# Layer 0's per-layer embedding computed in the even mixer ahead of its state scan, stored in DRAM and read back in the tail

## The chip, the cores and the metric

The program runs on one core of one Trainium2 chip. The metric is the device time of one execution in microseconds. The kernel before took 1391.22 us in the median of three runs (1390.14 to 1392.95). The engines are named as the profile names them: PE is the TensorE matmul engine (PEld its weight load), DVE the VectorE, ACT the ScalarE, POOL the GpSimd, SP the SyncE, whose queue issues nearly all DMAs here.

## The reference, cut to what matters

One inference step of a two-layer encoder over two groups of tokens that share the weights: 512 prompt rows and 32 sample rows, together T = 544 columns of width D = 1024, in float32. Layer 0 has the even mixer, layer 1 the odd one; each layer then has a causal ConvFFN and the gated per-layer embedding.

```python
for i in range(DEPTH):
    hn = rmsnorm(h, W['g_mix_pre'][i])
    # layer 0, the even mixer
    z = hn @ W['w_even_in'][j]
    gb, gc, xa, u = jnp.split(z, [A_WIDTH, 2 * A_WIDTH, 3 * A_WIDTH], axis=-1)
    yc, new_hist = causal_dwconv(gc * xa, hist, W['w_conv_a'][j])
    ya = gb * yc
    yb, nr, ni = s5_mixer(u, h0r, h0i, ...)      # complex diagonal scan, then GLU
    y = jnp.concatenate([ya, yb], axis=-1) @ W['w_even_out'][j]
    ...
    h = h + rmsnorm(y, W['g_mix_post'][i])
    hn = rmsnorm(h, W['g_ffn_pre'][i])
    up = hn @ W['w_ffn_up'][i]
    uc, new_f = causal_dwconv(up, fh, W['w_ffn_conv'][i])
    gt, val = jnp.split(uc, 2, axis=-1)
    y = (jax.nn.gelu(gt) * val) @ W['w_ffn_down'][i]
    h = h + rmsnorm(y, W['g_ffn_post'][i])
    h = h + jax.nn.sigmoid(h @ W['w_ple_gate'][i]) * (pe[i] @ W['w_ple'][i])
```

The change concerns the last factor, `pe[i] @ W['w_ple'][i]` (256 by 1024 weights), for layer 0. It depends on inputs alone.

## The kernel before

Activations lie with features on the partitions and the 544 columns in two halves of 256 and 288 (HALVES). Every float32 product is made from split operands: x = Xh + Xl and w = wh + wl in a rounded format, and each step of the contraction is three matmuls of 128 by 128 weights (L131 Xh with wh, L132 Xl with wh, L133 Xh with wl). A job (mm_job) is one output tile of 128 features for one half: with K = 8 steps 24 matmuls into one PSUM tile `ps`. A list of units (L53) gives the order in which weights are fetched: `prefetch` (L92) brings one unit over SP's queue into `raw`, ACT rounds it to `wh` (L107), DVE makes `wl` (L108).

`phase` (L166) runs the jobs of one matrix product: both halves, the second some jobs (delta) behind the first, and a consumer that evicts a job's PSUM tile a few jobs later (lag). Other work is written as generators in a task list; `run(n)`, called after each job, takes n steps of the list, so that the scan's small pieces are spread between jobs. The framework then reorders each engine's instructions somewhat before it fixes them: an engine issues in one fixed order, and waits on semaphores.

The even mixer (layer 0) has these parts in the program. The u jobs: phase of 4 tiles with c_u, 8 jobs in both halves. Then a shuffle of 16 DMAs brings u into the layout of the scan (L917). Then the scan is put on the task list (L897 to L915): prep_g makes G (L821) and PE transposes it (`tb`, L826); front multiplies u by the input matrix (`v`, L858) and scans on DVE (`rt` L867, `rg`, L875, `sp` L878); prep_c makes the output matrix Cm for five powers tau (products and sums `Tm` on DVE, L789 and L791, copied by ACT, L794); prep_t multiplies Cm by g on PE (`tp`, L837) and fills the matrix Tm (L840, L845); back applies Cm and Tm on PE (`yp`, L891 and L893). The a jobs: phase of 12 tiles with c_a, 24 jobs, which carry the scan's pieces between them. When both are through, the GLU (`GG`, L978) follows, and the output projection.

In the tail of each layer the ConvFFN's down jobs end with a residual for each half: a norm (`rp` on PE, L307 with ones and L314 with a transpose), and eight steps k on DVE and ACT, each of y (L338), h (L339), Xh (L323) and Xl (L325). Xh and Xl of a half feed the gate jobs, 24 matmuls each, one step of the contraction for each k. Between down and gate stands the embedding (L455 to L474): 16 jobs of two steps, 6 matmuls each, evicted by ACT with a factor 0.5 into `e` (L472).

Of the kernel before, what the change touches and what calls it, by code (L numbers as in the profile page):

```python
# [8 lines left out]
F32 = mybir.dt.float32  # L9
F32R = mybir.dt.float32r  # L10
# [41 lines left out]

def units():  # L53

    u = [("w_even_in", i, 8) for i in range(16)]
    u += [("w_glu", i, 8) for i in range(2)]
    u += [("w_even_out", i, 8) for i in range(8)]
    for layer in range(2):
        for p, (a, b) in enumerate(FF_PARTS):
            u += [("w_up%d" % layer, i, 8) for i in range(2 * a, 2 * b)]  # L60
            u += [("w_down%d_%d" % (layer, p), i, b - a) for i in range(8)]
        u += [("p", layer, 8)]
        u += [("w_ple%d" % layer, i, 8) for i in range(2)]
        u += [("w_gate%d" % layer, i, 8) for i in range(8)]
        if layer == 0:
            u += [("w_odd_in", i, 8) for i in range(21)]
            u += [("w_odd_out", i, 8) for i in range(8)]
    return u
# [3 lines left out]
def trunk_kernel(ctx: ExitStack, tc: tile.TileContext, A: dict):  # L72
# [4 lines left out]
    main = ctx.enter_context(tc.tile_pool(name="main", bufs=1))  # L77
    small = ctx.enter_context(tc.tile_pool(name="small", bufs=2))
    mm = ctx.enter_context(tc.tile_pool(name="mm", bufs=3, space=PSUM))


    ulist = units()
# [246 lines left out]
    def residual(half, h, y, st, gpost, gnext, rB=None):  # L329
# [18 lines left out]
            rB[half] = yield from s2.fin(D)  # L348
        waiting.discard(("r", half))


    def out_proj(layer, h, y, rB):

# [14 lines left out]
    def tail(layer, h, next_g):  # L368
# [2 lines left out]

        fs = ExitStack()
        ff = fs.enter_context(tc.tile_pool(name="ff%d" % layer, bufs=2))
        wscope(8 + 2 * NG + 24 + 11, fs.enter_context(tc.tile_pool(name="wf%d" % layer, bufs=4)))
        psc["extra"] = fs.enter_context(tc.tile_pool(name="fp%d" % layer, bufs=4, space=PSUM))
        psc["of"] = (7, 2)
        psc["st"] = fs.enter_context(tc.tile_pool(name="fs%d" % layer, bufs=1, space=PSUM))
# [11 lines left out]
        out_proj(layer, h, new_y(), rB)  # L389
        y = new_y()  # L390


        ps_r = ff.tile([128, 2, T - SEQ], F32, tag="psr", name="psr", bufs=1)
        nc.sync.dma_start(ps_r, A["ps"][layer])


        cg = [{}, {}]
# [6 lines left out]
        for p, (f0, f1) in enumerate(FF_PARTS):  # L404
            gt = [[ff.tile([128, 8, w], F32R, tag="g%d%s" % (half, s), name="g%s" % s, bufs=1)
                   for s in "hl"] for half, (_, w) in enumerate(HALVES)]

            def c_up(half, i, ps, f0=f0, gt=gt):
                w = HALVES[half][1]
                f, kind = f0 + i // 2, i % 2  # L410
                ct = f + NG * kind
                U = ff.tile([128, UW], F32, tag="U", name="U", bufs=3)
                vec.tensor_tensor(block_view(U, half)[2], like(ps, half), like(rB[half], half), op=OP.mult)  # L413
                history(U, half, hca[:, ct], hcs[:, layer, ct])
                if half == 0:
                    pool_e.tensor_copy(hca[:, ct], U[:, 256:258])  # L416
                t = ff.tile([128, T - 256], F32, tag="ct%d" % kind, name="t", bufs=2)
                t = t[:, :w]
                taps(U, half, t, lambda j: conv_w(j, ct))
                if half == 1:  # L420
                    ends(U, fout[:, layer, ct].rearrange("p (a b) -> p a b", a=2))
                if kind == 0:
                    act.activation(t, t, AF.Gelu_apprx_tanh)  # L423
                    cg[half][f] = t
                else:
                    g = cg[half].pop(f)
                    vec.tensor_tensor(g, g, t, op=OP.mult)  # L427
                    gh, gl = gt[half]
                    act.activation(gh[:, f - f0], g, AF.Copy)  # L429
                    vec.tensor_tensor(gl[:, f - f0], g, gh[:, f - f0], op=OP.subtract)  # L430

            phase(2 * (f1 - f0), 8, src_x, c_up, delta=6, rate=2, lag=6 if p == 0 else 1)

            def c_down(half, j, ps, p=p):
                yk = y[half][:, j]
                if p == 0:
                    act.activation(yk, ps, AF.Copy)
                else:
                    vec.tensor_tensor(yk, yk, ps, op=OP.add)  # L439
                if p == len(FF_PARTS) - 1:  # L440
                    st[half].add(yk)

            def a_down(half):
                def f():
                    task(residual(half, h, y[half], st[half], ("g_ffn_post", layer), None),
                         ("x", half), ("r", half))
                return f

            last = p == len(FF_PARTS) - 1
            phase(8, f1 - f0, lambda half, gt=gt: (gt[half][0], gt[half][1], 0), c_down, delta=6, rate=2, lag=4,  # L450
                  after=(a_down(0), a_down(1)) if last else (None, None))
        nc.sync.dma_start(A["o_ffn"][:, layer], fout[:, layer])


        us = take(3)  # L455
        prefetch(us[2])
        pA = [w_[:, :].rearrange("p (k t) c -> p k (t c)", k=2) for w_ in loaded[us[0]]]
        pB = [[ff.tile([128, T - 256], F32R, tag="ct%d" % i, name="pB", bufs=2) for k in range(2)] for i in range(2)]
        for k in range(2):
            for i in range(2):  # L460
                act.activation(pB[i][k][:, 0:256], pA[i][:, k, 256:512], AF.Copy)
            act.activation(pB[0][k][:, 256:], ps_r[:, k], AF.Copy)
            vec.tensor_tensor(pB[1][k][:, 256:], ps_r[:, k], pB[0][k][:, 256:], op=OP.subtract)
        emb = []
        for half, (c0, w) in enumerate(HALVES):
            e = ff.tile([128, 8, w], F32, tag="g%dh" % half, name="e", bufs=1)
            emb.append(e)
            xs = pA if half == 0 else pB
            for j in range(8):
                ps = ps_tile()  # L470
                mm_job(ps, us[1 + j // 4], range(2), xs[0], xs[1], 0, w, k0=2 * (j % 4))
                act.activation(e[:, j], ps[:, :w], AF.Copy, scale=0.5)  # L472
                run(j % 2)
        prefetch(us[2] + wsc["ring"])  # L474

        st = [Stat(0), Stat(1)]

# [40 lines left out]
    def mixer_even(h):  # L518
# [376 lines left out]
                           AF.Gelu_apprx_tanh)  # L895

        def scan():  # L897
            yield from prep_g(0)
            yield from prep_g(1)
            for s in range(10):  # L900
                if s >= 2:
                    back(s - 2)
                    yield
                if s == 5:
                    shuffle(True, (0, 1))
                if s < 8:
                    front(s)
                    yield
                    if s == 0:
                        yield from prep_c()  # L910
                    if s % 2 == 0:
                        yield from prep_t(s // 2)
                    elif s < 5:
                        yield from prep_g(s // 2 + 2)
            shuffle(True, (2, 3))  # L915
# [10 lines left out]
        task(discretize())  # L926
        phase(4, 8, src_x, c_u, delta=4, rate=3, lag=4)
        shuffle(False, (0, 1, 2, 3))
        task(scan())


# [423 lines left out]
        ms.close()  # L1355


    wscope(18)
    h = new_h()
    for half, (c0, w) in enumerate(HALVES):  # L1360
        for k0 in range(0, 8, 2 if half == 0 else 4):
# [157 lines left out]
```

## Time and profile before

| | us |
|---|---|
| runs | 1392.95, 1391.22, 1390.14 (median 1391.22) |
| profiled execution, its own time | 1392.53 |
| its span, first to last instruction | 1390.8 |
| PE busy | 1367.2 (98%) |
| DVE busy | 935.7 (67%) |
| ACT busy | 657.4 (47%) |
| mean granted PE clock | 0.996 of full speed |

The profile is one execution. A row of its timeline gives the start of an instruction (or of a run of equal ones), its length, the engine, the line of the kernel, the operation, the tiles written and read, the size and the count; in square brackets stands the idle time before it and what ended that. Matmuls overlap, so a job's length is read from the start of its first matmul to the start of the next job's first. Lines are those of the kernel before unless the kernel after is named.

### The profile page before, as it was taken

What the parts mean: (1) busy time and instruction counts of PE and PEld (TensorE: products, weight loads), DVE (VectorE), ACT (ScalarE), POOL (GpSimd) and SP (SyncE); (2) the same over time, 40 slices, a digit from 0 to 9 for tenths busy, and PEclk for the clock granted to TensorE, in tenths of its full rate; (3) what the DMA queues carried; (4) which work ended last, traced back from release to release, by engine and by line L of the source; (5) the groups of instructions that cost most, each with busy time, mean ns of one, the idle gap of its engine ahead of it and who ended that gap; (6) DMA issues with size and microseconds to landing.
All of it is one profiled execution on the core that took longest, in us unless ns stands there. A gap on an engine that the chain in (4) does not pass through costs nothing.

```text
span 1390.8 us, 27437 instructions
## 1 busy us (share of the span) xinstructions
PE 1367.2 (98%) x10859; PEld 1344.2 (97%) x10859; DVE 935.7 (67%) x1968; ACT 657.4 (47%) x1314; POOL 198.3 (14%) x621
## 2 busy tenths in 40 slices
PE   8899999999999999999999999999999999999998
PEld 8798999999999999999998998999999999999998
DVE  9998738983477546868655555479843676368682
ACT  6653545543344223445547755465433343234451
POOL 1000000431022201300131100012320123013000
PEclk9999999999999999999999999999999999999999
DMA  6322352232312231331332332331223123313321
GB/s 199 94 67 63 117 184 77 77 96 72 122 62 86 97 122 39 105 113 53 99 94 70 117 109 64 108 107 62 92 92 122 46 92 107 99 50 94 100 73 50
DMA packets 49376, 128.26 MB, mean 92 GB/s; under 512 B 8368, under 2 KB 19896, under 8 KB 48992
## 3 DMA queue, kind: packets, MB, share of 16 engines
q1 hardware_dynamic: 47456, 124.35, 28.0%
q0 software_dynamic: 1792, 2.17, 0.7%
q8 instruction: 85, 1.39, 0.4%
q14 instruction: 43, 0.35, 0.1%
HBM read 116.93 MB, written 4.76 MB: 88 GB/s over the span
## 4 chain that ended last, share of the span: by engine, by line
PE 87%; DVE 8%; ACT 2%; SPq 1%; DMA 1%; issue 1%; POOL 0%; ACTq 0%; DVEq 0%
PE ps L131 27%; PE ps L133 27%; PE ps L132 27%; DVE wl L108 1%; SPq L924 1%; PE av L1254 1%; PE rp L307 1%; DVE Xl L327 1%; PE pp L1243 1%; DVE rg L875 1%; DVE rt L877 1%; ACT wh L107 1%; PE sc L1230 1%; DVE y L338 0%; DMA h<-in_x 0%
## 5 line engine op out<-in xcount | busy, mean ns | idle before, releaser
L131 PE MATMUL ps<-Xh,wh 128*128 128x256 f32 (+1 forms) x2512 | 728.1, 290 | 1.8 <-ACT wh L107 1.1
L133 PE MATMUL ps<-Xh,wl 128*128 128x256 f32 (+1 forms) x2512 | 725.5, 289 | 2.0 <-DVE wl L108 2.0
L132 PE MATMUL ps<-Xl,wh 128*128 128x256 f32 (+1 forms) x2512 | 725.6, 289 | 0.8 <-DVE Xl L327 0.5
L131 PEld LDWEIGHTS ps<-Xh,wh 128*128 128x128 f32 x2512 | 473.9, 189 | 4.4 <-ACT wh L107 1.6
L132 PEld LDWEIGHTS ps<-Xl,wh 128*128 128x128 f32 x2512 | 474.7, 189 | 3.0 <-DVE Xl L327 1.2
L133 PEld LDWEIGHTS ps<-Xh,wl 128*128 128x128 f32 x2512 | 473.0, 188 | 2.5 <-DVE wl L108 2.4
L108 DVE TENSOR_TENSOR wl<-raw,wh 128x1024 fp32r<-128x1024 f32 (+2 forms) x214 | 256.9, 1201 | 151.3 <-ACT wh L107 149.5
L107 ACT ACTIVATE wh<-raw 128x1024 fp32r<-128x1024 f32 (+2 forms) x214 | 222.1, 1039 | 248.3 <-PE ps L132 232.9
L131 PE MATMUL ps<-gh,wh 128*128 128x288 f32 (+1 forms) x704 | 203.5, 289 | 0.0
L133 PE MATMUL ps<-gh,wl 128*128 128x288 f32 (+1 forms) x704 | 203.4, 289 | 0.0
L132 PE MATMUL ps<-gl,wh 128*128 128x288 f32 (+1 forms) x704 | 202.5, 288 | 0.0
L132 PEld LDWEIGHTS ps<-gl,wh 128*128 128x128 f32 x704 | 133.5, 190 | 0.0
L131 PEld LDWEIGHTS ps<-gh,wh 128*128 128x128 f32 x704 | 133.0, 189 | 0.0
L133 PEld LDWEIGHTS ps<-gh,wl 128*128 128x128 f32 x704 | 132.9, 189 | 0.0
L278 ACT ACTIVATE t<-U,prm 128x256 f32<-128x256 f32 (+1 forms) x176 | 90.4, 517 | 71.0 <-DVE U L413 67.5
L279 DVE SCALAR_TENSOR_TENSOR t<-U,prm,t 128x256 f32<-128x256 f32 (+1 forms) x176 | 87.2, 498 | 34.9 <-ACT t L278 34.7
L413 DVE TENSOR_TENSOR U<-ps,rB 128x256 f32<-128x256 f32 (+1 forms) x176 | 76.6, 437 | 23.9 <-PE ps L133 19.8
L280 DVE SCALAR_TENSOR_TENSOR t<-U,prm,t 128x256 f32<-128x256 f32 (+1 forms) x176 | 87.5, 501 | 4.5
L416 POOL COPY hca<-U 128x2 f32<-128x2 f32 x88 | 24.3, 277 | 366.2 <-DVE U L413 366.1
L423 ACT ACTIVATE t<-t 128x288 f32<-128x288 f32 (+1 forms) x88 | 37.7, 429 | 81.6 <-DVE t L280 81.5
L439 DVE TENSOR_TENSOR y<-y,ps 128x256 f32<-128x256 f32 (+1 forms) x64 | 27.9, 436 | 62.0 <-PE ps L133 62.0
L429 ACT ACTIVATE gh<-t 128x288 fp32r<-128x288 f32 (+1 forms) x88 | 37.4, 425 | 67.3 <-DVE t L427 67.3
(272 smaller groups left out, 1376.7 us busy)
## 6 DMA issues: line engine op xcount, KB each, us to landing
raw<-in_w_up SPq DMA_DIRECT2D x88, 512.0 KB, 3.4
raw<-in_w_down SPq DMA_DIRECT2D x32, 512.0 KB, 3.4
raw<-in_w_odd_in SPq DMA_DIRECT2D x21, 512.0 KB, 3.6
raw<-in_w_gate SPq DMA_DIRECT2D x16, 512.0 KB, 4.0
raw<-in_w_even_in SPq DMA_DIRECT2D x15, 512.0 KB, 3.7
raw<-in_w_down SPq DMA_DIRECT2D x16, 384.0 KB, 3.1
raw<-in_w_even_out SPq DMA_DIRECT2D x8, 512.0 KB, 4.0
raw<-in_w_odd_out SPq DMA_DIRECT2D x8, 512.0 KB, 3.5
```

Of the source, the lines that this page charges most:

```text
L107: act.activation(wh[:, k], raw[:, k], AF.Copy)
L108: vec.tensor_tensor(wl[:, k], raw[:, k], wh[:, k], op=OP.subtract)
L131: pe.matmul(ps[:, :n], wh[:, k0 + k, :], h_, start=(i == 0), stop=False)
L132: pe.matmul(ps[:, :n], wh[:, k0 + k, :], l_, start=False, stop=False)
L133: pe.matmul(ps[:, :n], wl[:, k0 + k, :], h_, start=False, stop=(i == last))
L278: act.activation(t, v[2], AF.Copy, scale=w(2))
L279: vec.scalar_tensor_tensor(t, v[1], w(1), t, op0=OP.mult, op1=OP.add)
L280: vec.scalar_tensor_tensor(t, v[0], w(0), t, op0=OP.mult, op1=OP.add)
L413: vec.tensor_tensor(block_view(U, half)[2], like(ps, half), like(rB[half], half), op=OP.mult)
L423: act.activation(t, t, AF.Gelu_apprx_tanh)
L429: act.activation(gh[:, f - f0], g, AF.Copy)
L439: vec.tensor_tensor(yk, yk, ps, op=OP.add)
```

## The change

The embedding of layer 0 moves out of the tail. Its units (the input `p` and two of `w_ple0`) come after the four units of the u jobs. A function `embed` now holds the products for both layers. For layer 0 it is called in the even mixer after the u jobs and the shuffle, ahead of `task(scan())` and of the a jobs; with halves of 288 and 256 columns; each of its 16 jobs is evicted by ACT into a small tile `e` (three buffers), stored by an SP DMA into a DRAM tensor `emb0`, and takes one step of the task list. In the tail of layer 0 two DMAs read `emb0` back into the tiles that the gate uses. Layer 1 keeps its embedding where it was.

`scan` begins with three empty steps of the task list, so its pieces come three steps later. In the last down phase of layer 0 the consumer runs two jobs behind instead of four.

```diff
@@ -52,15 +52,19 @@
 
 def units():
 
-    u = [("w_even_in", i, 8) for i in range(16)]
+    u = [("w_even_in", i, 8) for i in range(4)]
+    u += [("p", 0, 8)]
+    u += [("w_ple0", i, 8) for i in range(2)]
+    u += [("w_even_in", i, 8) for i in range(4, 16)]
     u += [("w_glu", i, 8) for i in range(2)]
     u += [("w_even_out", i, 8) for i in range(8)]
     for layer in range(2):
         for p, (a, b) in enumerate(FF_PARTS):
             u += [("w_up%d" % layer, i, 8) for i in range(2 * a, 2 * b)]
             u += [("w_down%d_%d" % (layer, p), i, b - a) for i in range(8)]
-        u += [("p", layer, 8)]
-        u += [("w_ple%d" % layer, i, 8) for i in range(2)]
+        if layer == 1:
+            u += [("p", 1, 8)]
+            u += [("w_ple1", i, 8) for i in range(2)]
         u += [("w_gate%d" % layer, i, 8) for i in range(8)]
         if layer == 0:
             u += [("w_odd_in", i, 8) for i in range(21)]
@@ -77,6 +81,8 @@
     main = ctx.enter_context(tc.tile_pool(name="main", bufs=1))
     small = ctx.enter_context(tc.tile_pool(name="small", bufs=2))
     mm = ctx.enter_context(tc.tile_pool(name="mm", bufs=3, space=PSUM))
+    dram = ctx.enter_context(tc.tile_pool(name="dram", bufs=1, space=bass.MemoryType.DRAM))
+    emb0 = dram.tile([128, 8, T], F32, tag="emb0", name="emb0")
 
 
     ulist = units()
@@ -348,6 +354,25 @@
             rB[half] = yield from s2.fin(D)
         waiting.discard(("r", half))
 
+    def embed(ps_, pB, n0, put):
+
+        us = take(3)
+        prefetch(us[2])
+        pA = [w_[:, :].rearrange("p (k t) c -> p k (t c)", k=2) for w_ in loaded[us[0]]]
+        m = SEQ - n0
+        for k in range(2):
+            for i in range(2):
+                act.activation(pB[i][k][:, 0:m], pA[i][:, k, n0:SEQ], AF.Copy)
+            act.activation(pB[0][k][:, m:T - n0], ps_[:, k], AF.Copy)
+            vec.tensor_tensor(pB[1][k][:, m:T - n0], ps_[:, k], pB[0][k][:, m:T - n0], op=OP.subtract)
+        for n, (c0, w) in enumerate(((0, n0), (n0, T - n0))):
+            xs = pB if n else pA
+            for j in range(8):
+                ps = ps_tile()
+                mm_job(ps, us[1 + j // 4], range(2), xs[0], xs[1], 0, w, k0=2 * (j % 4))
+                put(n, j, c0, w, ps[:, :w])
+        prefetch(us[2] + wsc["ring"])
+
 
     def out_proj(layer, h, y, rB):
 
@@ -371,7 +396,7 @@
 
         fs = ExitStack()
         ff = fs.enter_context(tc.tile_pool(name="ff%d" % layer, bufs=2))
-        wscope(8 + 2 * NG + 24 + 11, fs.enter_context(tc.tile_pool(name="wf%d" % layer, bufs=4)))
+        wscope(8 + 2 * NG + 24 + (11 if layer else 8), fs.enter_context(tc.tile_pool(name="wf%d" % layer, bufs=4)))
         psc["extra"] = fs.enter_context(tc.tile_pool(name="fp%d" % layer, bufs=4, space=PSUM))
         psc["of"] = (7, 2)
         psc["st"] = fs.enter_context(tc.tile_pool(name="fs%d" % layer, bufs=1, space=PSUM))
@@ -389,9 +414,10 @@
         out_proj(layer, h, new_y(), rB)
         y = new_y()
 
-
-        ps_r = ff.tile([128, 2, T - SEQ], F32, tag="psr", name="psr", bufs=1)
-        nc.sync.dma_start(ps_r, A["ps"][layer])
+        if layer:
+
+            ps_r = ff.tile([128, 2, T - SEQ], F32, tag="psr", name="psr", bufs=1)
+            nc.sync.dma_start(ps_r, A["ps"][layer])
 
 
         cg = [{}, {}]
@@ -447,31 +473,25 @@
                 return f
 
             last = p == len(FF_PARTS) - 1
-            phase(8, f1 - f0, lambda half, gt=gt: (gt[half][0], gt[half][1], 0), c_down, delta=6, rate=2, lag=4,
+            phase(8, f1 - f0, lambda half, gt=gt: (gt[half][0], gt[half][1], 0), c_down, delta=6, rate=2,
+                  lag=2 if last and layer == 0 else 4,
                   after=(a_down(0), a_down(1)) if last else (None, None))
         nc.sync.dma_start(A["o_ffn"][:, layer], fout[:, layer])
 
 
-        us = take(3)
-        prefetch(us[2])
-        pA = [w_[:, :].rearrange("p (k t) c -> p k (t c)", k=2) for w_ in loaded[us[0]]]
-        pB = [[ff.tile([128, T - 256], F32R, tag="ct%d" % i, name="pB", bufs=2) for k in range(2)] for i in range(2)]
-        for k in range(2):
-            for i in range(2):
-                act.activation(pB[i][k][:, 0:256], pA[i][:, k, 256:512], AF.Copy)
-            act.activation(pB[0][k][:, 256:], ps_r[:, k], AF.Copy)
-            vec.tensor_tensor(pB[1][k][:, 256:], ps_r[:, k], pB[0][k][:, 256:], op=OP.subtract)
-        emb = []
-        for half, (c0, w) in enumerate(HALVES):
-            e = ff.tile([128, 8, w], F32, tag="g%dh" % half, name="e", bufs=1)
-            emb.append(e)
-            xs = pA if half == 0 else pB
-            for j in range(8):
-                ps = ps_tile()
-                mm_job(ps, us[1 + j // 4], range(2), xs[0], xs[1], 0, w, k0=2 * (j % 4))
-                act.activation(e[:, j], ps[:, :w], AF.Copy, scale=0.5)
+        emb = [ff.tile([128, 8, w], F32, tag="g%dh" % half, name="e", bufs=1) for half, (_, w) in enumerate(HALVES)]
+        if layer == 0:
+            for half, (c0, w) in enumerate(HALVES):
+                nc.sync.dma_start(emb[half], emb0[:, :, c0:c0 + w])
+        else:
+            pB = [[ff.tile([128, T - 256], F32R, tag="ct%d" % i, name="pB", bufs=2) for k in range(2)]
+                  for i in range(2)]
+
+            def put_e(n, j, c0, w, ps):
+                act.activation(emb[n][:, j], ps, AF.Copy, scale=0.5)
                 run(j % 2)
-        prefetch(us[2] + wsc["ring"])
+
+            embed(ps_r, pB, 256, put_e)
 
         st = [Stat(0), Stat(1)]
 
@@ -895,6 +915,8 @@
                            AF.Gelu_apprx_tanh)
 
         def scan():
+            for _ in range(3):
+                yield True
             yield from prep_g(0)
             yield from prep_g(1)
             for s in range(10):
@@ -926,6 +948,19 @@
         task(discretize())
         phase(4, 8, src_x, c_u, delta=4, rate=3, lag=4)
         shuffle(False, (0, 1, 2, 3))
+
+
+        ps_r = s5.tile([128, 2, T - SEQ], F32, tag="psr", name="psr")
+        nc.sync.dma_start(ps_r, A["ps"][0])
+        pB = pt([128, 2, 2, 256], "pB").bitcast(F32R)
+
+        def put_e(n, j, c0, w, ps):
+            e = small.tile([128, T - 256], F32, tag="sq", name="e", bufs=3)[:, :w]
+            act.activation(e, ps, AF.Copy, scale=0.5)
+            nc.sync.dma_start(emb0[:, j, c0:c0 + w], e)
+            run(1)
+
+        embed(ps_r, [[pB[:, i, k] for k in range(2)] for i in range(2)], 288, put_e)
         task(scan())
 
 
@@ -1355,7 +1390,7 @@
         ms.close()
 
 
-    wscope(18)
+    wscope(21)
     h = new_h()
     for half, (c0, w) in enumerate(HALVES):
         for k0 in range(0, 8, 2 if half == 0 else 4):
```

Line numbers of the kernel after: matmuls L137 to L139, `rp` L313 and L320, `tb` L846, `tp` L857, `v` L878, `Cm` copies L814, evictions of the embedding `e` L959, `so` L900.

PE at the start of the even mixer, before: the u jobs end with the first row, then six a jobs with `tb` and `v` between them, then `tp`.

```order
L133 MATMUL ps<-Xh,wl 128x288
L131 MATMUL ps<-Xh,wh 128x256 [waits DVE_49,PE_49,Activation_49]
...
L826 MATMUL tb<-cst,G 128x128 [waits PE_49,Activation_49]
...
L858 MATMUL v<-UUh,Bm 128x137 x2
...
L837 MATMUL tp<-Cm,g_707 32x128 [waits Activation_49]
L837 MATMUL tp<-Cm,g_707 32x128 x7
```

The same place after: behind the u jobs stand the embedding's jobs (`ps<-wh` for the first 288 columns, `ps<-pB` for the other 256), then `tp`, and only then the first a job.

```order
L139 MATMUL ps<-Xh,wl 128x288
L137 MATMUL ps<-wh 128x288 [waits DVE_49,Activation_49]
...
L137 MATMUL ps<-pB,wh 128x256 [waits Activation_49]
...
L846 MATMUL tb<-cst,G 128x128 [waits Activation_49]
...
L139 MATMUL ps<-pB,wl 128x256
L857 MATMUL tp<-Cm,g_957 32x128 [waits Activation_49]
L857 MATMUL tp<-Cm,g_957 32x128 x5
L137 MATMUL ps<-Xh,wh 128x256 [waits Activation_49]
```

What moved: before, 6 of the 24 a jobs stand ahead of the first `tp` on PE; after, none does, and the embedding's 96 matmuls stand there instead.

ACT at the copies of Cm that `tp` waits for, before: two copies for each power tau, close together.

```order
L794 ACTIVATE Cm<-Tm 64x32x16 [waits DVE_49]
L794 ACTIVATE Cm<-Tm 64x32x16
L107 ACTIVATE wh<-raw 128x1024 [waits DMAHW5_49,PE_49]
L794 ACTIVATE Cm<-Tm 64x32x16 [waits DVE_49]
L794 ACTIVATE Cm<-Tm 64x32x16
L880 ACTIVATE so<-sp 128x2x2x2 [waits DVE_49]
```

After, evictions `e` of the embedding stand between them, each waiting for a DMA (the store that frees its buffer).

```order
L814 ACTIVATE Cm<-Tm 64x32x16 [waits DVE_49]
L959 ACTIVATE e<-ps 128x256 [waits DMAHW6_49,Activation_49]
L959 ACTIVATE e<-ps 128x256 [waits DMAHW7_49,Activation_49]
L959 ACTIVATE e<-ps 128x256 [waits DMAHW0_49,PE_49,Activation_49]
L900 ACTIVATE so<-sp 128x2x2x2 [waits DVE_49]
L814 ACTIVATE Cm<-Tm 64x32x16
```

What moved: three evictions of the embedding and one copy of the scan's state stand between the two Cm copies of one power.

PE from the last down jobs of layer 0 to the gate, after (the names ps_7748 and ps_7711 are the last two down tiles, ps_7810 and ps_7843 the first two gate tiles); before, the norm's second `rp` stands behind the last down job and the embedding's 96 matmuls follow it.

```order
L139 MATMUL ps_7674<-gh_6410,wl_7234 128x288
L320 MATMUL rp_7663<-cst_75,rc_7668 128x128 [waits Pool_49]
...
L139 MATMUL ps_7711<-gh_6410,wl_7276 128x288
...
L139 MATMUL ps_7748<-gh_6410,wl_7320 128x288
L137 MATMUL ps_7810<-Xh_96,wh_7520 128x256 [waits Activation_49]
L138 MATMUL ps_7810<-Xl_97,wh_7520 128x256 [waits DVE_49]
L139 MATMUL ps_7810<-Xh_96,wl_7521 128x256
L137 MATMUL ps_7810<-Xh_96,wh_7520 128x256 [waits Activation_49]
L137 MATMUL ps_7843<-Xh_96,wh_7572 128x256
```

What moved: `rp` stands two jobs ahead of the end of down, the gate follows down at once, and its first five tiles take turns, one step of the contraction after another.

## Rows read from the trace of the kernel before

**Rows 1.** The page: busy time, share and instructions of each engine.
```profile
PE 1367.2 (98%) x10859; PEld 1344.2 (97%) x10859; DVE 935.7 (67%) x1968; ACT 657.4 (47%) x1314; POOL 198.3 (14%) x621
```

**Rows 2.** Windows: stretch, length, busy PE, PEld, DVE, ACT, POOL, clock, DMA, GB/s.
```profile
60.00:70.00 10.00, 5.52 (x31) 4.37 (x30) 10.00 (x18) 6.04 (x9) 0.11 (x1) 0.69 0.00 0
38.50:69.70 31.20, 25.43 (x194) 24.01 (x192) 31.20 (x72) 20.70 (x40) 0.21 (x2) 0.91 0.33 89
69.70:156.05 86.35, 81.39 (x641) 79.23 (x641) 72.64 (x137) 40.28 (x90) 0.82 (x8) 0.99 0.25 74
624.20:636.50 12.30, 12.30 (x100) 12.30 (x99) 11.68 (x29) 10.98 (x28) 0.00 (x0) 1.00 0.29 88
```

**Rows 3.** PE timeline: two a jobs at full clock (three boundaries).
```profile
91.13 0.37 PE L131 MATMUL ps<-Xh,wh 128*128 128x256 f32 x1
...
94.05 0.30 PE L131 MATMUL ps<-Xh,wh 128*128 128x288 f32 x1
...
97.24 1.10 PE L858 MATMUL v<-UUh,Bm 128*128 128x137 f32 x8
```

**Rows 4.** PE timeline: first a job; the wait for Cm and after it.
```profile
38.56 0.28 PE L131 MATMUL ps<-Xh,wh 128*128 128x256 f32 x1
...
66.19 3.62 PE L837 MATMUL tp<-Cm,g 128*32 128x128 f32 x16 [4.48 <-ACT Cm L794]
69.74 0.58 PE L131 MATMUL ps<-Xh,wh 128*128 128x256 f32 x1
...
70.74 0.29 PE L132 MATMUL ps<-Xl,wh 128*128 128x256 f32 x1
...
83.71 1.94 PE L837 MATMUL tp<-Cm,g 128*32 128x128 f32 x16
```

**Rows 5.** ACT and DVE timelines: what that wait hangs on, and two evictions.
```profile
64.86 1.27 ACT L794 ACTIVATE Cm<-Tm 64x512 f32<-64x512 f32 x2 [1.92 <-DVE Tm L791]
64.14 0.69 DVE L791 TENSOR_TENSOR Tm<-Tm 128x512 f32<-128x512 f32 x1
44.89 0.42 DVE L941 TENSOR_TENSOR gct<-ps,rB 128x256 f32<-128x256 f32 x1
626.68 0.39 ACT L472 ACTIVATE e<-ps 128x256 f32<-128x256 f32 x1 [0.28 <-PE ps L133]
```

**Rows 6.** PE timeline: later waits, last `yp`, GLU's first matmul; DVE: the last GG.
```profile
80.59 1.09 PE L826 MATMUL tb<-cst,G 128*128 128x128 f32 x8 [0.70 <-ACT G L821]
101.72 1.09 PE L826 MATMUL tb<-cst,G 128*128 128x128 f32 x8 [0.89 <-ACT G L821]
116.18 0.47 PE L893 MATMUL yp<-UUh,Tm 128*128 128x137 f32 x2 [1.78 <-DMA Tm<-Tm]
134.91 0.47 PE L891 MATMUL yp<-sp,Cm 128*128 128x137 f32 x2 [1.37 <-DVE sp L878]
136.28 0.40 PE L893 MATMUL yp<-UUh,Tm 128*128 128x137 f32 x2
156.05 0.28 PE L131 MATMUL ps<-GG,wh 128*128 128x274 f32 x1
149.65 0.73 DVE L978 TENSOR_TENSOR GG<-UUh,GG 128x548 fp32r<-128x548 f32 x1
```

**Rows 7.** PE and DVE timelines: down's end, embedding, gate; the residual's first and last step.
```profile
624.12 0.38 PE L314 MATMUL rp<-cst,rc 128*128 128x128 f32 x2
624.25 0.36 PE L131 MATMUL ps<-wh 128*128 128x256 f32 x1
636.48 0.28 PE L131 MATMUL ps<-Xh,wh 128*128 128x256 f32 x1
626.42 0.48 DVE L338 SCALAR_TENSOR_TENSOR y<-y,prm,rB 128x256 f32<-128x256 f32 x1
635.79 0.76 DVE L325 TENSOR_TENSOR Xl<-h,Xh 128x256 fp32r<-128x256 f32 x2
```

## The prediction

> **What bounds the kernel now.** I read the page first, for the busy shares: PE 1367.2 us of a span of 1390.8, 98%, against DVE 67% and ACT 47% [rows 1]. PE stands still for 23.6 us in the whole span, so a change pays only if it shortens PE's work, or the time in which PE waits or runs at the lower clock. Moving the embedding changes no matmul: the number and sizes of PE's instructions stay. The question is only which PE waits it fills and which it makes.
>
> Next I read the windows of the even mixer, to see whether it has waits that are worth filling. It has one place: in 60 to 70 PE is busy for 5.52 of 10 us at a granted clock of 0.69 [rows 2]. The PE timeline shows why: `tp` starts at 66.19 after 4.48 us of waiting for ACT's copy of Cm, and its 16 matmuls take 3.62 us where 16 later ones take 1.94 [rows 4]. One step back, ACT's copy at 64.86 waited for the sum `Tm` on DVE (64.14 plus 0.69) [rows 5], and DVE is busy for 31.20 of the 31.20 us from 38.50 to 69.70 [rows 2]. So up to about 66 the even mixer is bound by DVE (E, `v` products, `Tm` products), and `tp` comes when DVE lets it, whatever PE has done by then. What PE does while it waits is its own choice: before, it did six a jobs there.
>
> Last I read the end of layer 0's down phase, to see what the embedding does in its old place. It runs from 624.25 to the gate's first matmul at 636.48 [rows 7], with PE busy all through [rows 2], and behind it DVE makes the residual of half 0 (626.42 to 636.55), which the gate needs.
>
> **The change part by part, on PE.**
>
> *The a jobs ahead of `tp`.* In the new order none of the six stands there. A job of 256 columns takes 94.05 − 91.13 = 2.92 us, one of 288 takes 97.24 − 94.05 = 3.19 [rows 3]. Four and two of them: 11.68 + 6.38 = 18.1 us of PE work that used to run while DVE was behind, and that now runs after `tp`. That is +18.1, unless `tp` itself comes sooner.
>
> *When the a jobs begin.* DVE's work ahead of the sum for `tp` stays, but for two evictions of a jobs, at 0.42 us like the `gct` row [rows 5]. On ACT three `e` evictions at 0.39 [rows 5], 1.2 us, now stand between the two Cm copies. So `tp` starts at about 66.19 − 0.8 + 1.2 = 66.6. Six of its eight instructions stand ahead of the first a job. At the speed of the first `tp` row they take 6/8 of 3.62 = 2.7 us, and the first a job begins at 69.3; the other two cost 0.5 later, and together this is 0.1 after the 69.74 of before [rows 4]. At the speed of the second row (1.94) they take 1.5, the a jobs begin at 68.1 (68.6 with the other two), and the first a job doesn't lose the 0.5 us that its start lost at the low clock (69.74 to 70.74 for four matmuls of 0.12): that is −1.7. I take the middle, −0.8, since what runs ahead of `tp` now comes in short pieces of six matmuls, each of which waits for an eviction. If the stores of `e` hold ACT up further, it is later: I allow +2.
>
> The row shows that PE, after 4.5 us of waiting, was at a granted clock of 0.69 in that stretch and did `tp` at about half speed [rows 2, 4]. The Trainium skill, page "TensorE: Matmul & The Clock Gate", section "HAM oscillation — how this bites in real kernels", says that a PE which waits between short bursts falls back to the lower rate, so that each burst begins slowly. That speaks against this change, which makes such bursts of the last embedding jobs: by that rule the value at the low clock, +0.1 in place of −0.8, is the one to take, and the sum would be 0.9 higher. What it does if it spreads further is a rival below.
>
> *The embedding in its new place.* Its 96 matmuls took 636.48 − 624.25 = 12.2 us [rows 7]. In the new place they stand before a `tp` that comes at its own time, and PE has 38.56 to 66.6, 28 us [rows 4], for them and for 16 `tb` and 8 `v`, four groups of 1.1 us or less (the `tb` rows) [rows 6]: 12.2 + 4.4 = 16.6. They cost nothing there, and PE's idle time in this stretch grows from 31.20 − 25.43 = 5.8 us [rows 2] to 28 − 16.6, some 11 to 12. The embedding goes out of the tail: −12.2.
>
> *The waits after `tp`.* Before, four are left in the mixer: 0.70, 0.89, 1.78 and 1.37, together 4.7 us [rows 6]. After `tp` PE now has ten a jobs before the first `yp` instead of three, so DVE and ACT get seven jobs, some 20 us, of lead; from there on the scan's pieces stand as many jobs apart as before. The two waits of `tb` for G hang on DVE and ACT alone and should go, −1.6. The other two hang on a `v` a fixed number of jobs before, and stay. Bounds: 0 and −4.7.
>
> *GLU's start.* From the last `yp` to GLU's first matmul PE had 156.05 − 136.28 = 19.8 us of work, and GG was ready at 149.65 + 0.73 = 150.4, 14.1 us after that `yp` [rows 6]. Now 4.2 jobs stand between, 12.9 us. The first GLU job needs the last GG only in its last three matmuls, and so I put +0.5 here (0 to +2).
>
> *Gate's start.* The embedding covered the residual; now the gate follows down at once. In return `rp` stands two of the 18-matmul jobs ahead of down's end (36 times 0.133 = 4.8 us). Before, DVE began the residual 2.3 us after `rp` (624.12 to 626.42) and was done 10.1 us later [rows 7]. Now it begins 2.5 us before down's end, its first step is out at about the end, and its last 7.6 us after it; with the two evictions of down that now come in between, some 10. The gate's first five tiles take turns, so each step k gives PE 15 matmuls of 0.12, 1.8 us, while a step comes every 1.3. PE waits a little at the first steps only: +1.0. Bounds: 0, and +7.6, if no matmul of the gate could run before the last step.
>
> *Edits at nothing.* Stores of `emb0` (16 more DMAs on SP) and two loads back stand where SP has long gaps. The evictions of `e` are the same number on ACT as in the tail. The subtractions for pB on DVE are now two of 32 columns ahead of `tp`, an eighth of the width of the 0.42 us row [rows 5]; DVE's sum for `tp` carries them, and the allowance of +2 above.
>
> *The sum:* 18.1 − 0.8 − 12.2 − 1.6 + 0.5 + 1.0 = +5.0. The profiled execution took 1392.5 (a span of 1390.8 and 1.7 around it), 1.3 above the median of the runs; it would take 1397.5. On the median of 1391.2 that is 1396.2.
>
> Put in one sentence: the embedding fills a wait that six a jobs already filled, with 12 us of work instead of 18, and the other 6 come later.
>
> **The rivals.** I count 0.2%, 2.8 us, as no change.
>
> (a) *The a jobs catch up.* DVE has the lead, all four later waits vanish, the a jobs start as early as with the full clock, the edges of GLU and gate cost nothing: 18.1 − 1.7 − 4.7 − 12.2 = −0.5; with DVE done sooner by another 1 us, −1.5: 1389.7 to 1390.7, no change. For it: DVE is busy for only 72.64 of 86.35 us after 69.70 [rows 2]. Against it: the spacing of the scan's pieces is the same.
>
> (b) *The embedding does fill waits (the other side, faster).* If `tp` can come far sooner because DVE, freed of a-job evictions, reaches the sum `Tm` earlier, the wait of 4.48 and the slow stretch (3.62 − 1.94 and 0.5) go too. With a `tp` at 59.5 instead of 66.6 the a jobs begin at 61.0, 8.7 sooner than before, and 18.1 − 8.7 − 4.7 − 12.2 = −7.5, 1383.7. It decides from a `tp` at about 64 on (a jobs at 65.7, −4.0), where the sum passes −2.8 with the later waits gone. Against it: only two evictions of 0.33 us stand ahead of that sum on DVE [rows 5], and DVE has no gap to give.
>
> (c) *Short bursts at the low clock.* PE waits before each of the last embedding jobs, runs them and `tp` at half speed, ACT gets its tiles later, and the a jobs begin at 71 to 72 rather than 68.9: +2 to +3 more, 1398.2 to 1399.2. For it: 0.69 in 60 to 70 [rows 2].
>
> (d) *The gate waits for the residual.* The turn-taking doesn't cover it, +7.6 instead of +1.0: 1402.8. For it: DVE also has weights to split there. Against it: the new order.
>
> **How the numbers follow.** Forecast 0.47 (1393 to 1399 on its own); (a) 0.20; (b) 0.10; (c) 0.13; (d) 0.10. Slower by over 0.2% (above 1394.0): most of the forecast's case (0.38), (c) and (d), 0.61 together. Within 0.2%: the rest of the forecast (0.09) and most of (a) (0.17), 0.26. Faster (below 1388.4): (b) and the rest of (a), 0.13. The range for 8 times in 10 leaves out most of (b) and of (d): 1387 to 1402.
>
> **What would show it.** In the profile of the changed kernel: PE from 38.6 to about 69 with some 12 us of waiting, `tp` at 66 to 67 behind ACT's Cm copies, a granted clock below 1 there; the first a job at about 69; GLU's first matmul some 15 us later than 156.05, near 171; the later `tb` waits gone, the `yp` waits still there; the gate's first matmul near 640 instead of 636.48, with small waits for DVE's Xl in its first steps. The forecast is wrong if GLU starts before 166, or if `tp` starts before 64, or if the gate shows one wait of several us.

## The result and the profile after

The changed kernel took 1401.39 us in the median (1399.22 to 1403.20), before 1390.68 in the same comparison: a ratio of 1.0070, 95% interval 1.0057 to 1.0083, slower by some 10 us. The forecast was slower, by 5, which lies below that interval (7.9 to 11.5 us). The profiled execution of the changed kernel took 1402.32 us, its span 1400.6, 9.8 above that of before.

Where the time went is read by comparing the same instruction in both traces. GLU's first matmul stood at 156.05 [rows 6], now at 175.17: +19.1. The gate's first stood at 636.48 [rows 7], now at 642.57: +6.1. The odd mixer's first scores (`pick`) stood at 717.31, now at 725.78: +8.5, and the end at +9.8. So the start of GLU is 19.1 later, the stretch from there to the gate gives 13.0 back (12.4 of it at the embedding's old place), and the gate phase and the odd mixer take 3.7 more.

The PE timeline of the kernel after, from the first embedding job to the first a job, and GLU's first matmul:

```profile
39.80 0.29 PE L137 MATMUL ps<-wh 128*128 128x288 f32 x1
...
50.02 1.09 PE L846 MATMUL tb<-cst,G 128*128 128x128 f32 x8 [0.89 <-ACT G L841]
...
54.40 1.65 PE L846 MATMUL tb<-cst,G 128*128 128x128 f32 x8 [2.54 <-ACT G L841]
...
59.60 2.19 PE L878 MATMUL v<-UUh,Bm 128*128 128x137 f32 x8 [2.18 <-DVE rt L887]
63.24 0.58 PE L137 MATMUL ps<-pB,wh 128*128 128x256 f32 x1 [1.45 <-ACT e L959]
...
67.04 0.41 PE L139 MATMUL ps<-pB,wl 128*128 128x256 f32 x1
67.89 0.58 PE L137 MATMUL ps<-pB,wh 128*128 128x256 f32 x1 [0.44 <-ACT e L959]
...
70.46 1.50 PE L857 MATMUL tp<-Cm,g 128*32 128x128 f32 x12
71.89 0.38 PE L137 MATMUL ps<-Xh,wh 128*128 128x256 f32 x1
...
175.17 0.28 PE L137 MATMUL ps<-GG,wh 128*128 128x274 f32 x1
```

`tp` comes at 70.46 and no longer waits: in its place PE waits for G, for `rt` and for the evictions `e`. The last six embedding jobs run from 63.24 on, and the first three of them (18 matmuls, 17 steps from 63.24 to 67.04) take 0.22 us a matmul, where one of this width takes 0.12 at full clock [rows 3]; the last three are at 0.12 again from 68.47 on. The windows show the same (columns as in [rows 2]):

```profile
50.00:60.00 10.00, 5.01 (x26) 4.25 (x27) 10.00 (x23) 7.26 (x14) 0.11 (x1) 0.74 0.62 165
60.00:70.00 10.00, 8.11 (x41) 7.49 (x41) 9.35 (x16) 5.81 (x13) 0.00 (x0) 0.58 0.25 84
39.00:71.90 32.90, 24.48 (x149) 21.92 (x147) 31.93 (x72) 25.20 (x53) 0.24 (x3) 0.79 0.54 155
71.90:175.15 103.25, 99.19 (x789) 96.91 (x789) 78.20 (x142) 45.07 (x100) 0.84 (x8) 1.00 0.26 78
```

Up to the a jobs the granted clock is 0.79, against 0.91 before, and PE is idle for 8.4 of 32.9 us.

Not all of the 19.1 arises here. The first embedding job begins at 39.80, where the first a job of before began at 38.56 [rows 4], so the u jobs ended 1.2 us later in this execution. Its window 10 to 20 shows a clock of 0.83, that of before 1.00:

```profile
10.00:20.00 10.00, 8.28 (x56) 7.87 (x55) 8.13 (x23) 8.06 (x15) 0.93 (x1) 0.83 0.94 322
10.00:20.00 10.00, 8.02 (x63) 7.36 (x62) 9.71 (x29) 8.61 (x17) 0.93 (x1) 1.00 0.98 330
```

The profile of the kernel before with the down lag of 2, whose start is that of before, shows 0.83 there too, and its first a job at 39.96; the changed kernel without the scan delay shows 1.00 there, and its first embedding job at 38.48. So I don't count the 1.2 to the change. From the first job behind the u jobs to GLU it is 117.5 us before and 135.4 after, 17.9 more.

Why the six jobs came so late is in SP's queue (issues and their time) and in ACT's timeline of the same stretch:

```profile
44.93 10.41 SPq L946 DMA_DIRECT2D UUh<-UUh  x16
55.44 0.53 SPq L960 DMA_DIRECT2D emb<-e  x1
56.07 0.89 SPq L960 DMA_DIRECT2D emb<-e  x2
...
63.22 5.94 SPq L960 DMA_DIRECT2D emb<-e  x6
```

```profile
61.49 1.27 ACT L814 ACTIVATE Cm<-Tm 64x512 f32<-64x512 f32 x2 [1.04 <-DVE Tm L811]
62.78 0.99 ACT L959 ACTIVATE e<-ps 128x288 f32<-128x288 f32 x3
66.00 1.06 ACT L113 ACTIVATE wh<-raw 128x1024 fp32r<-128x1024 f32 x1 [2.23 <-PE ps L138]
66.96 0.61 ACT L814 ACTIVATE Cm<-Tm 64x512 f32<-64x512 f32 x1
67.48 0.90 ACT L959 ACTIVATE e<-ps 128x256 f32<-128x256 f32 x3
68.50 0.63 ACT L814 ACTIVATE Cm<-Tm 64x512 f32<-64x512 f32 x1
```

The fourth store is issued at 55.44, right behind the 16 DMAs of the shuffle. Until it has landed, the seventh eviction has no buffer among the three. By the median of 1.9 us from issue to landing of these stores that is at about 57.3, an estimate; the other 5 us are ACT's fixed order, in which the eviction stands behind the Cm copies at 61.49 and runs at 62.78. So long the PSUM tiles that the next jobs need stay full, and the a jobs, which come behind the embedding in the program, stand behind it.

In the gate phase and behind it (PE timeline, then a window):

```profile
667.62 0.40 PE L137 MATMUL ps<-Xh,wh 128*128 128x288 f32 x1 [0.29 <-ACT Xh L329]
...
707.20 0.54 PE L320 MATMUL rp<-cst,rc 128*128 128x128 f32 x3 [0.84 <-POOL rc L317]
...
740.18 0.39 PE L1265 MATMUL sc<-KA,QA 128*128 128x256 f32 x1 [1.17 <-ACT S L1207]
```

```profile
740.00:750.00 10.00, 9.82 (x61) 8.91 (x61) 5.34 (x15) 8.04 (x25) 0.33 (x1) 0.83 0.11 32
```

The first two waits are new. The third is in both kernels with the same length; behind it this execution of the kernel after shows a granted clock of 0.83 over 10 us, 1.7 us lost, and that of before does not.

### The profile page after: what moved, and what is told of

Its sections match the earlier page's. It is cut to its first block, busy times and chain, and to the rows that moved or that the text cites. A ratio compares the mean times of both kernels' runs of the same rounds, so it can differ in the third digit from the quotient of the medians.

```text
span 1400.6 us, 27486 instructions
## 1 busy us (share of the span) xinstructions
PE 1373.8 (98%) x10859; PEld 1348.9 (96%) x10859; DVE 936.8 (67%) x1968; ACT 655.4 (47%) x1314; POOL 198.3 (14%) x621
## 4 chain that ended last, share of the span: by engine, by line
PE 87%; DVE 8%; ACT 2%; issue 1%; POOL 1%; SPq 1%; DMA 1%; ACTq 0%; POOLq 0%; DVEq 0%
PE ps L137 27%; PE ps L139 27%; PE ps L138 27%; DVE wl L114 2%; PE av L1289 1%; DVE Xl L333 1%; PE rp L313 1%; DVE y L344 1%; PE pp L1278 1%; DVE h L345 1%; PE sc L1265 1%; SPq L946 0%; ACT wh L113 0%; DVE rt L887 0%; PE rp L320 0%
## 5 line engine op out<-in xcount | busy, mean ns | idle before, releaser
L137 PE MATMUL ps<-Xh,wh 128*128 128x256 f32 (+1 forms) x2512 | 726.5, 291 | 1.9 <-ACT Xh L1028 1.0
L139 PE MATMUL ps<-Xh,wl 128*128 128x256 f32 (+1 forms) x2512 | 725.2, 289 | 2.7 <-DVE wl L114 2.7
L137 PEld LDWEIGHTS ps<-Xh,wh 128*128 128x128 f32 x2512 | 473.6, 189 | 4.8 <-issue 1.6
L139 PEld LDWEIGHTS ps<-Xh,wl 128*128 128x128 f32 x2512 | 473.4, 189 | 3.1 <-DVE wl L114 3.1
L137 PE MATMUL ps<-gh,wh 128*128 128x288 f32 (+1 forms) x704 | 203.6, 289 | 0.0
L139 PE MATMUL ps<-gh,wl 128*128 128x288 f32 (+1 forms) x704 | 203.4, 289 | 0.0
L137 PEld LDWEIGHTS ps<-gh,wh 128*128 128x128 f32 x704 | 133.0, 189 | 0.0
L139 PEld LDWEIGHTS ps<-gh,wl 128*128 128x128 f32 x704 | 132.9, 189 | 0.0
```

The source lines that it names most:

```text
L137: pe.matmul(ps[:, :n], wh[:, k0 + k, :], h_, start=(i == 0), stop=False)
L139: pe.matmul(ps[:, :n], wl[:, k0 + k, :], h_, start=False, stop=(i == last))
```

## The experiments

Theory 1, formed on the trace after: the a jobs are held up because the embedding's stores stand behind the shuffle on SP. Theory 2: DVE sets the time, and the embedding costs its 12.2 us wherever it stands in the mixer. Ratios are to the kernel before, run beside each; a difference in us that follows a ratio is read from it and can differ by up to 1 from that of the medians.

**Stores on ACT's queue.**

```diff
-            nc.sync.dma_start(emb0[:, j, c0:c0 + w], e)
+            nc.scalar.dma_start(emb0[:, j, c0:c0 + w], e)
```

> The changed kernel with the 16 stores of the embedding issued by ACT instead of SP, so that none stands behind the 16 DMAs of the shuffle. Theory 1 (the stores wait on SP behind the shuffle, hold the three buffers of the embedding, and with them PSUM and all the a jobs): PE now has all 16 embedding jobs and 8 a jobs ahead of tp, no wait of several us before it; GLU starts at 160 to 165 instead of 175.2, and the time falls from 1401.4 by 10 to 15, to 1386 to 1391. Theory 2 (DVE sets the time of tp and of what follows it, and the embedding fills nothing wherever its stores go): GLU at 172 to 176, time 1398 to 1402.

Measured 1394.33 us, 1.0020 (1.0012 to 1.0029): 7 us of some 10 gone, with 3 less than theory 1 said, so the time missed its range; GLU starts at 165.3, at the edge of theory 1's, where theory 2 had 172 to 176. Eight a jobs stand ahead of `tp`, as theory 1 said. The windows show no wait for Cm and the full clock:

```profile
50.00:60.00 10.00, 9.04 (x73) 8.64 (x73) 9.73 (x22) 6.87 (x14) 0.00 (x0) 1.00 0.79 217
60.00:70.00 10.00, 10.00 (x84) 10.00 (x83) 8.63 (x18) 9.44 (x19) 0.11 (x1) 1.00 0.42 145
```

PE is busy for 10.00 of 10 where it was 5.52 before [rows 2] and 8.11, at 0.58, after the change.

**The shuffle on ACT's queue.**

```diff
-                    nc.sync.dma_start(a if back_ else b, b if back_ else a)
+                    (nc.sync if back_ else nc.scalar).dma_start(a if back_ else b, b if back_ else a)
```

> The changed kernel with the 16 DMAs of the first shuffle issued by ACT, the stores left on SP. Theory 1 (stores behind the shuffle): the same fall as with the stores on ACT, to 1386 to 1392, with stores landing within some 3 us of their issue. Theory 2 (DVE sets it): 1398 to 1402. A theory by which the three buffers or the stores themselves are too slow, whatever stands ahead of them on the queue: no fall here, 1399 to 1402.

Measured 1405.10, 1.0097 (1.0083 to 1.0111): a miss for theory 1 as it was put. The trace says why. ACT's queue issued the 16 DMAs and nothing else for 10 us, and PE waited for the eviction behind them:

```profile
45.66 10.18 ACTq L946 DMA_DIRECT2D UUh<-UUh  x15
55.89 0.72 ACT L775 ACTIVATE E<-E 128x252 f32<-128x252 f32 x2 [10.45 <-DMA UUh<-UUh]
```

```profile
59.50 0.61 PE L137 MATMUL ps<-wh 128*128 128x288 f32 x1 [12.44 <-ACT e L959]
```

Whatever stands behind those 16 issues waits, be it a store on SP or an eviction on ACT. The run moved the block rather than taking it away, so its time can't tell the theories apart. Its order does say something: with no shuffle ahead of the stores on SP, eight a jobs stand ahead of `tp` here too, which comes at 95.52:

```profile
95.52 1.93 PE L857 MATMUL tp<-Cm,g 128*32 128x128 f32 x16
```

**Stores on POOL's queue** (`nc.gpsimd.dma_start` in the first edit).

> The changed kernel with the 16 stores of the embedding issued by POOL, so that neither SP's shuffle nor ACT's evictions stand on the same queue. PE has 16 embedding jobs and 8 a jobs ahead of tp, as with the stores on ACT. Theory 1 (the stores' place behind the shuffle on SP costs 7 us): 1392 to 1396, GLU at 163 to 167. Rival (what helped with the stores on ACT was ACT's own order, not the queue they left): 1399 to 1402.

Measured 1396.33, 1.0028 (1.0017 to 1.0040), GLU at 169.3. This is 0.3 above theory 1's range and 3 below the rival's (GLU is 2 later than theory 1 had it): leaving SP helps with either queue, and with both eight a jobs stand ahead of `tp`. PE's waits for `e` are 3.2 us here, 2.3 with the stores on ACT; the stores take 2.5 to 2.9 us to land instead of the 1.8 to 1.9 from SP.

**Down lag 4 again** (`lag=4` for the last down phase).

> The changed kernel with the last down phase of layer 0 running four jobs behind again. Theory 1: the mixer is untouched (GLU at 175 to 176), and the residual begins two jobs, 4.8 us, later, so that the gate waits for it for 1 to 5 us: 1402 to 1406. Rival (the lag of two costs by itself): faster than 1401.4 by 1 to 3.

Measured 1405.50, 1.0101 (1.0087 to 1.0115), as theory 1 said. One wait at the gate's start:

```profile
648.59 1.06 PE L313 MATMUL rp<-ones,sq 128*128 128x1 f32 x6 [2.82 <-DVE sq L304]
```

**Down lag 2 in the kernel before** (the same line, the other way).

> The kernel before with the last down phase of layer 0 two jobs behind instead of four, and nothing else; the embedding still covers the residual. Theory 1: the lag matters only where the gate follows down at once, so no change here: 1390 to 1393. Rival (the shorter lag makes PE wait for PSUM in the down phase): slower by 2 to 4.

Measured 1394.19, 1.0014 (1.0005 to 1.0023): slower by 2, outside theory 1's range and at the edge of the rival's, though not by its mechanism: the down phase shows no wait. A wait of 0.73 of `rp` for POOL's `rc` appears at 636.50, ahead of the gate; it isn't the one of the changed kernel, which comes some 65 us behind the gate's start. What makes the 2 us is otherwise open.

**No scan delay** in the changed kernel.

```diff
-            for _ in range(3):
-                yield True
```

> The changed kernel without the three empty steps at the start of the scan. Theory 1: the order ahead of tp stays (16 embedding jobs, no a job), tp at 70 to 71, time within 2 us of 1401.4. Rival (the delay is what pushes the a jobs behind tp or makes the later waits): 1393 to 1398.

Measured 1398.45, 1.0053 (1.0039 to 1.0067): 2.4 us better, more than theory 1 allowed and less than the rival, though the two intervals (from 1.0039 and up to 1.0083) overlap. `tp` and GLU come earlier (68.94 and 172.1), with the same waits ahead of `tp`; 1.3 us of that was there already at the first embedding job (38.48 for 39.80), ahead of the edit, which leaves 1.8 at GLU. **No delay and stores on ACT** together:

> The changed kernel with the stores of the embedding on ACT's queue and without the delay of the scan: 16 embedding jobs and five a jobs ahead of tp. If the two edits add up (7 us and some 2.5 us): 1391 to 1392.5. Theory 1 as stated (the delay matters only through the order ahead of tp, which has no gap to fill here): 1393 to 1396.

Measured 1391.43, 0.9992 (0.9983 to 1.0001): in the total they add up, and this interval lies clear of the one with the delay (1.0012 to 1.0029). The profiles show only 0.8 us of it between the first embedding job and GLU. The other 2.5 lies behind it, where the run with the delay waits 0.84 us at the output projection's start and has a clock of 0.83 in 180 to 190, and this run has neither.

**The scan delay in the kernel before**, and nothing else.

> The kernel before with the three empty steps at the start of the scan and nothing else. PE has nine a jobs ahead of tp instead of six. Theory 1: the wait for Cm (4.5 us) and most of the slow stretch go, tp comes at 70 to 72; what is gained there is lost in part at GLU, since the scan ends three jobs later: 1386 to 1391. Rival (the late scan makes GLU wait for its last GG): 1392 to 1396.

Measured 1386.94, 0.9967 (0.9955 to 0.9980): faster by 4.6 us than before, and the fastest whole kernel of all. Nine a jobs fill the wait for Cm, and GLU starts at 149.15 without waiting (a wait of 0.37 for GG comes at 153.71):

```profile
69.24 1.93 PE L837 MATMUL tp<-Cm,g 128*32 128x128 f32 x16 [0.24 <-ACT Cm L794]
...
88.01 1.09 PE L826 MATMUL tb<-cst,G 128*128 128x128 f32 x8 [2.71 <-ACT G L821]
```

The wait of 4.48 is 0.24, `tp` takes 1.93 instead of 3.62 [rows 4], and a part (2.71) comes back at a later `tb`.

**The embedding left out**, which prices the tail alone.

```diff
-        embed(ps_r, [[pB[:, i, k] for k in range(2)] for i in range(2)], 288, put_e)
+        for j in range(8):
+            nc.gpsimd.dma_start(emb0[:, j], Xl[:, j].bitcast(F32))
```

(The diff leaves out the embedding's units and the three empty steps of the scan, which go with it.)

> The changed kernel without the embedding of layer 0: its matmuls, weights and evictions are left out, and emb0 is filled from a tile that is there anyway, over POOL's queue; the scan has no delay, so that the mixer has the order of before. It prices the tail alone. Theory 1: GLU starts at 156 to 158, the 12.2 us of the embedding are gone from the tail, and 2.4 to 4 us come back between the gate's start and the odd mixer's attention, as in the changed kernel: 1381.5 to 1384. Rival (without the embedding's cover the gate waits for the residual): one wait of 4 to 8 us at the gate, 1386 to 1388.

Measured 1384.58, 0.9945 (0.9931 to 0.9959): 7.7 us less than before, where I had 1381.5 to 1384. The run is not as clean as it was meant to be. GLU is 3.2 later than before, and 3.8 had been lost ahead of the mixer's a jobs, the first of which begins at 42.34 instead of 38.56 (PE timeline). The DMAs that fill `emb0` run just there, in the u jobs (POOL timeline):

```profile
42.34 0.28 PE L135 MATMUL ps<-Xh,wh 128*128 128x256 f32 x1
```

```profile
29.07 3.27 POOL L957 DMA_DIRECT2D emb<-Xl  x6
```

Whether they are the cause isn't shown; part is a clock of 0.83 in 10 to 30. So the 7.7 puts the tail too low. The old place gives 12.4, of which 2.5 comes back between the gate's start and `pick`: the tail gives about 10, not 12.2. The rival's wait of 4 to 8 us isn't there.

**The embedding behind six a jobs.**

```diff
-        phase(12, 8, src_x, c_a, delta=2, after=(a_a(0), a_a(1)), rate=2, lag=2)
+        phase(3, 8, src_x, c_a, delta=2, rate=2, lag=2)
+        embed(ps_r, ..., 288, put_e)
+        phase(9, 8, src_x, lambda half, i, ps: c_a(half, i + 3, ps), delta=2, after=(a_a(0), a_a(1)), rate=2, lag=2)
```

(The order of the units and the steps of the task list are changed to fit.)

> The changed kernel with the a phase cut in two: three tiles (six a jobs) stand ahead of the embedding, nine behind it, and the scan takes one step of the task list after every fourth embedding job; stores on SP as in the change. PE has six a jobs and 12 of the 16 embedding jobs ahead of tp. Theory 1 (the loss is the order: a jobs held up behind stores that stand behind the shuffle): no wait for Cm ahead of tp and no slow stretch there, GLU at 160 to 164, time 1384 to 1389. Theory 2 (the mixer is bound by DVE and the embedding adds its full 12.2 us wherever it stands): GLU at 167 to 170, 1393 to 1396.

Measured 1391.70, 0.9998 (0.9989 to 1.0007): GLU at 163.2 as theory 1 said, 12 us earlier than in the changed kernel and 7.1 later than before, but the time missed its range. What the trace shows for it is a wait at the output projection's start and a slow stretch behind it, whose 3.3 us alone would bring the time into that range, at its upper end; that is one execution, and whether the others have it isn't shown:

```profile
178.72 0.38 PE L137 MATMUL ps<-Xh,wh 128*128 128x256 f32 x1 [1.39 <-ACT Xh L1030]
```

```profile
180.00:190.00 10.00, 9.65 (x57) 9.33 (x57) 5.17 (x8) 4.78 (x10) 0.00 (x0) 0.67 1.02 343
```

## Why the prediction was right, and where it was off

The sign held, and so did the core of the mechanism: six a jobs had filled PE's wait, the embedding fills it with less, and the a jobs come later by what they take. The size did not: 10.7 us on the medians against 5.0. The 1401.39 lies in the range of 1387 to 1402 only by 0.6, outside the 1393 to 1399 that the forecast had by itself; the range held because it was drawn wide enough for rivals (c) and (d). Of the signs that the prediction gave, GLU came at 175 instead of near 171, and `tp` at 70.5 behind the last embedding job, not at 66 to 67 behind the Cm copies. Term by term, on the profiled executions:

| term | forecast | measured |
|---|---|---|
| six a jobs displaced | +18.1 | all 24 stand behind `tp` |
| a jobs begin | −0.8 | +2.15 (71.89 for 69.74), 1.24 of it in the u jobs |
| a jobs' start to GLU, beyond the 18.1 | −1.1 (−1.6 and +0.5) | −1.1 (103.28 − 86.31 − 18.06) |
| GLU's start in all | +16.2 | +19.1 |
| embedding out of the tail | −12.2 | −12.4 (down's last matmul to the gate's) |
| GLU to down's end | 0 | −0.7 |
| gate's start | +1.0 | no wait at the start, +2.4 until `pick` |
| odd mixer and behind | 0 | +1.3 |
| in all | +5.0 | +9.8 |

The first three terms add up to GLU's +19.1 by the way they are read, since the third is what is left over. The step that failed in size is "When the a jobs begin". I let `tp` come at 66.6, on the ground that DVE alone decides it, and cost the stores at nothing, "where SP has long gaps". SP has no gap there: 16 DMAs stand ahead, 10.41 us, and the last six embedding jobs ran late and ahead of `tp`, the first three of them at half speed. That is much of what rival (c) described, with the a jobs at 71 to 72, and 1398.2 to 1399.2 as its time; I gave it 0.13. Its `tp` at half speed didn't come (1.50 us for 12 matmuls). The allowance of +2 for "if the stores hold ACT up further" covers most of it. The runs with the stores elsewhere show that this place costs 6 to 7 us, more than the term was off: with the stores on ACT or POOL, or the shuffle off SP, eight a jobs stand ahead of `tp`. So the displaced jobs, which I took from the order as given, were themselves due to the queue. That three buffers are part of it follows from the order; a run with more of them wasn't made.

One slip changes nothing: for the stretch ahead of `tp` the prediction counts 8 `v`, where the trace has 16; its four groups and 4.4 us are right.

The low clock: the trace shows 0.74 in 50 to 60 and 0.58 in 60 to 70, where PE waited five times between short pieces. The Trainium skill ("TensorE: Matmul & The Clock Gate", section "HAM oscillation — how this bites in real kernels") says that a PE which waits between bursts falls back to the lower rate, so that each burst starts slow. The 0.22 us a matmul agree with that, though in the page's case the waits are longer than the bursts, and here waits of 0.25 to 2.54 us stand between bursts of 0.5 to 4.2.

The later waits and GLU's start came out near the forecast in sum, and partly by luck: the `tb` waits gave 0.5 instead of 1.6, the `yp` waits 0.4 instead of nothing, and GLU lost nothing where I had put 0.5. Of the two `tb` waits that I let go one is left (1.10 at 127.20); the two `yp` waits stayed, as forecast (1.41 and 1.32), and GLU starts without a wait.

The gate's start: taking turns did hide the residual (the gate follows down's last matmul by 0.13 us, without a wait); I looked for the loss at the first steps, but 2.4 us come later, of which 0.84 is the wait of `rp` for POOL and 0.29 one for Xh, with their restarts. The runs without the embedding in the tail have the same 2.3 to 2.5 (1.8 with lag 4, which waits ahead of the gate). The wait of `rp` goes with the embedding's move, not with the lag: all nine profiles without the embedding in the tail have it at this place (0.81 to 0.84), lag 4 among them, and none of the three with it. Why POOL is late there, and what makes up the rest, I have not settled.

The odd mixer's 1.3 us need not be the change's: profiles with and without it show such a stretch near 720 to 750 (before with the scan delay, before with lag 2) or none (no scan delay, embedding left out). Such stretches are also why GLU's place in single profiles is good to about 1.5 us only.

What the change bundles, then: with the stores off SP and no delay, it is 125.7 us from the first embedding job to GLU, against 117.5 from the first a job before. So the embedding costs some 8 us in the mixer even there, the tail gives about 10, and the time is that of before within its interval (0.9983 to 1.0001): in no arrangement tried here did the move gain. The scan delay, which the prediction did not price by itself, gains 4.6 us alone, where it puts three more a jobs ahead of `tp`. In the changed kernel, where none gets there, it costs some 2.4, and with the stores on ACT 3.9 by the ratios.

## What to carry to other kernels

Before moving work into a wait, see what fills that wait now, and price the move by the difference. Of a step with DMAs, look at what stands ahead of them on their queue and which buffers they release: 16 issues of 0.65 us stood ahead of the stores that free the buffers here, and behind the buffers the whole order of PE. Test the parts of a change alone: the small part was the one that paid.

## What the runs showed of the hardware

A queue that issues DMAs holds up what stands behind it, and on ACT that is compute: 15 issues of the shuffle took 10.18 us, during which ACT did nothing else. A window of 10 us with a granted clock of 0.83, 1.7 us lost, appeared in most profiles, at different places (10 to 30, 180 to 190, 230 to 250, 720 to 750), before and after alike.
